# Stationary operands read with a step of two elements, and moving operands at other distances from them, in a conformer/state-space block

## The chip, the cores and the metric

The kernel runs on one core of one Trainium2 chip. The metric is the device time of one execution in microseconds. Five engines matter: TensorE (PE, matrix products, whose load of the stationary operand the profile lists apart as PEld), VectorE (DVE), ScalarE (ACT), GpSimd (POOL) and SyncE (SP), which here only issues DMAs.

## The reference, cut to what matters

One block of 512 tokens by 1024 features, everything in fp32. With `D = 1024`:

```python
h = rms_norm(x, mix_pre_g)
proj = h @ w_in                        # GLU halves, z, x/B/C, dt, gates
gates = sigmoid(proj[..., OFF_GATE:] + gate_b)
conv_out = conformer_conv_branch(...)  # GLU, 31-tap conv, layer norm, silu, @ pw_w
ssm_out = ssd_branch(...)              # 4-tap convs, chunked state space, group norm, @ ssm_out_w
mixed = (g_conv * conv_out + g_ssm * ssm_out) @ w_out
x = x + rms_norm(mixed, mix_post_g)
h = rms_norm(x, ffn_pre_g)
gt, up = split(h @ w_gate_up)
x = x + rms_norm((silu(gt) * up) @ w_down, ffn_post_g)
```

## The kernel before

**Three products for one.** An fp32 operand is held as two float32r tiles, a rounded high part and the remainder (`whi`/`wlo` for weights, `hhi`/`hlo`, `ehi`/`elo`, `yh`/`yl`, `vhi`/`vlo`, `mh`/`ml`, `fh`/`fl` for activations). `mm3` (lines 160 to 164) issues three matmuls per pair of tiles: high by high, stationary high by moving low, stationary low by moving high. Nearly all TensorE time is in these 5,448 matmuls (1,816 calls, the first strip's written out at lines 442 to 444).

**Weights.** `ORDER` lists 128 x 1024 pieces of the weights, laid out on the host by `_layout`. `w_raw` loads one from DRAM through the SP queue (five buffers, three ahead), `w_part` makes the high part with ACT and the low part with DVE, or with ACT and an accumulating DMA on the POOL queue. A piece is a strip of 128 output columns with its eight k tiles of 128 rows side by side; `proj` (line 190) takes columns `k*P` to `(k+1)*P` as the stationary operand and all 512 tokens as the moving one.

**The stages, in order.** (1) `val`/`glu` strips 0 to 7, strips 0 to 2 with `ehi`/`elo` as moving operand, the others with `hhi`/`hlo`; a 31-tap convolution follows on DVE, its taps fed out between later matmuls by `conv_some`, which ties each tap to the PE's progress. (2) Eight groups of the state-space branch: strips `x` (two), `B`, `C`, and `z` in `proj_z`, where the tokens in `hhi`/`hlo` are stationary and 256 columns of weights move; between them small fp32 matmuls (`s1` to `s4`) and the output product `ssm_out`, weights stationary and `yh`/`yl` moving. (3) Gates `gs` and `gc`, the layer norm of the convolution, and `pw` with `vhi`/`vlo` moving. (4) The product with `w_out` (`tm_step`): tokens in `mt` stationary, weights moving, then residual and norm in `residual`, and `transposed`, which writes the halves `b11` to `t4` in the `mov` tiles. (5) Gate and up projections in a seven-product form: 22 steps of 256 columns, `product` (line 848) takes a combination of weight quarters as stationary operand and one of seven combinations of activation halves (256 tokens) as moving one; four k tiles and three matmuls each. (6) The product with `w_down`: tokens in `fh`/`fl` stationary, weights moving.

**Where the tiles lie.** Taken modulo 512 bytes within a partition, the weight tiles (`whi`, `wlo`, `chi`, `clo`, `dhi`, `dlo`) begin at 160, and so do `ehi`, `elo`, `yh`, `yl`, `vhi`, `vlo`, the `mt` tiles, all `mov` tiles and the `f` tiles; `hhi` and `hlo` begin at 480. The unnamed tiles `place` and `mp_place` hold space only. The distance from a stationary to a moving operand, modulo 512 bytes, is thus 0 everywhere but with `hhi`/`hlo`: 320 where they move, 192 where they stand still in `proj_z`.

**Order of the work.** The Tile framework sets the order on each engine from the order of the calls, the explicit `keep_in_program_order`, `issue_after` and `not_before` edges, and the free buffers. [...]

Of the kernel before, what the change touches and what calls it, by code (L numbers as in the profile page):

```python
# [10 lines left out]
F32 = mybir.dt.float32  # L11
# [7 lines left out]
P = 128  # L19
# [77 lines left out]
ORDER += [("wd", _i) for _i in range(NF)]  # L97


def b3(ap, n):  # L100

    return ap.unsqueeze(len(ap.shape)).to_broadcast(list(ap.shape) + [n])
# [3 lines left out]
def block_kernel(ctx: ExitStack, tc: tile.TileContext, x, xT, prm, hp, gp, w, out):  # L106
# [83 lines left out]
    def proj(ps, wt, rhs=None):  # L190
        wh, wl = wt
        rhi, rlo = rhs or ([hhi[:, k, :] for k in range(NK)], [hlo[:, k, :] for k in range(NK)])
        for k in range(NK):
            c = slice(k * P, (k + 1) * P)
            mm3(ps, wh[:, c], wl[:, c], rhi[k], rlo[k], k == 0, k == NK - 1)

    sp = mid.enter_context(tc.tile_pool(name="mid", bufs=1))
# [227 lines left out]
    for j in range(NK):  # L425
        if j == EARLY:
            proj_z0()
            time_steps()
        if j == DT2:
            running_sums()  # L430
            L = {0: make_L(0)}
        if j == 1:
            pv, pg = [ydp.tile([P, T], F32, tag=f"yd{n}", name=f"p{n}_1") for n in range(2)]
        else:
            pv, pg = mm_tile(f"pv{j}"), mm_tile(f"pg{j}")
        early = (ehi, elo) if j < EARLY else None
        if j == 0:
            for k in range(NK):
                for ps, n in ((pv, "val"), (pg, "glu")):
                    wh, wl = w_get(n, 0)  # L440
                    c = slice(k * P, (k + 1) * P)
                    in_order(pe.matmul(ps, wh[:, c], ehi[k], start=k == 0, stop=False))
                    pe.matmul(ps, wl[:, c], ehi[k], start=False, stop=False)
                    pe.matmul(ps, wh[:, c], elo[k], start=False, stop=k == NK - 1)
            first = pv, pg
            continue
        proj(pv, w_get("val", j), early)
        if j == 1:
            with tc.issue_after(mark["pe"].ins):
                norm_x()  # L450
        proj(pg, w_get("glu", j), early)
        if j == 1:
            norm_to_all()
            gated(0, *first, True)
            norm_h()
        gated(j, pv, pg, early)
        if j >= EARLY - 1:
            conv_some(TAPS_GLU)
# [129 lines left out]
    def s4(g):  # L588
        s = st[g]
        yz = s["y"].rearrange("p c h d -> p c (h d)")  # L590
        if g % 2 == 0:
            ys[g // 2] = [ssd.tile([P, 4, T], F32R, tag=f"y{n}", name=f"y{n}{g}") for n in "hl"]
        yh, yl = ys[g // 2]
        for e in range(2):
            ps = aux_tile(f"pyT{g}_{e}")
            for c in range(NT):
                pe.transpose(ps[:, c * P : (c + 1) * P], yz[:, c, e * P : (e + 1) * P], ident)
            act.activation(yh[:, 2 * (g % 2) + e, :], ps, AF.Copy, scale=col("norm_g", 2 * g + e))
            dve.scalar_tensor_tensor(
                out=yl[:, 2 * (g % 2) + e, :], in0=ps, scalar=col("norm_g", 2 * g + e),  # L600
                in1=yh[:, 2 * (g % 2) + e, :].bitcast(F32), op0=ALU.mult, op1=ALU.subtract,
            )
        del st[g]

    def ssm_out(p, quarters):

        yh, yl = ys[p]
        for q in quarters:
            wh, wl = w_get("so", 4 * p + q)
            for i in (2 * q, 2 * q + 1):  # L610
                ps = mm_tile(f"pso{p}_{i}")
                for k in range(4):
                    c = slice(k * 256 + (i % 2) * P, k * 256 + (i % 2 + 1) * P)
                    mm3(ps, wh[:, c], wl[:, c], yh[:, k, :], yl[:, k, :], k == 0, k == 3)
                if p == 0:
                    act.copy(so[i], ps)
                else:
                    dve.tensor_tensor(out=so[i], in0=ps, in1=so[i], op=ALU.add)
# [53 lines left out]
    br.close()  # L672

    vp = mid.enter_context(tc.tile_pool(name="vT", bufs=1))
    vhi = vp.tile([P, NK, T], F32R, name="vhi")
    vlo = vp.tile([P, NK, T], F32R, name="vlo")
    gc = vp.tile([P, NK, T], F32, name="gc")
# [53 lines left out]
    mp = mix.enter_context(tc.tile_pool(name="mp", bufs=1, side="right"))  # L731
    M2 = T // 2
    mt = [[mp.tile([P, NK, M2], F32R, tag=f"m{n}{p}", name=f"m{n}{p}") for p in "hl"] for n in range(2)]
    mp.tile([P, 80], F32, name="mp_place")
    wo0 = seq[("wo", 0)]
    for i in range(NK):
        pw = mm_tile(f"ppw{i}")
# [52 lines left out]
    HB = T // 2  # L790
    KB = NK // 2
    MOV = ("b11", "b21", "b22", "t1", "t2", "t3", "t4")
    mov = {n: [h2p.tile([P, KB, HB], F32R, name=f"{n}{p}") for p in "hl"] for n in MOV}
    w2 = h2.enter_context(tc.tile_pool(name="w2", bufs=1))

    pm = ExitStack()
# [51 lines left out]
    def product(ps, u, wn, mn, start):  # L848

        wh, wl = forms[u, wn]  # L850
        mh, ml = mov[mn]
        for k in range(KB):
            c = slice(k * P, (k + 1) * P)
            mm3(ps, wh[:, c], wl[:, c], mh[:, k], ml[:, k], start and k == 0, k == KB - 1, not start)

    xrs, xgs = {}, {}

    def residual(t, ps):

        xr = pmp.tile([P, D], F32, tag="xr", name=f"xr{t}")  # L860
        nc.scalar.dma_start(xr, x[t * P : (t + 1) * P, :])
        mg = pmp.tile([P, D], F32, tag="mg", bufs=1, name=f"mg{t}")
        ss = []
        for n, c in enumerate(cols2):
            ss.append(mean_sq(ps[n], pmp, f"a{t}", n))
            dve.tensor_tensor(out=mg[:, c], in0=ps[n], in1=gpost0[:, c], op=ALU.mult)
        rs = factor(ss, f"a{t}")
        ss = []
        for n, c in enumerate(cols2):
            dve.scalar_tensor_tensor(out=xr[:, c], in0=mg[:, c], scalar=rs, in1=xr[:, c], op0=ALU.mult, op1=ALU.add)  # L870
            ss.append(mean_sq(xr[:, c], pmp, f"b{t}", n))
        rs = factor(ss, f"b{t}")
        dg = pmp.tile([P, P], F32, tag="dg", name=f"dg{t}")
        mark["dg"] = dve.tensor_scalar(out=dg, in0=ident, scalar1=rs, scalar2=None, op0=ALU.mult)
        xrs[t] = xr, dg
        nc.scalar.dma_start(x2d[t * P : (t + 1) * P, :], xr)

    def transposed(t):

        tok = slice((t // 2) * P, (t // 2 + 1) * P)  # L880
        xr, dg = xrs[t]
        xg = []
        for n in range(2):
# [44 lines left out]
    steps = [(t, k) for k in range(4) for t in (0, 1)] + [(t, k) for t in (0, 1) for k in range(4, NK)]  # L928
    steps += [(t, k) for t in (2, 3) for k in range(NK)]
    for t, k in steps:  # L930
        (mh, ml), tok = mt[t // 2], slice(t % 2 * P, (t % 2 + 1) * P)
        tm_step(ps, t, k, NK, mh[:, k, tok], ml[:, k, tok], split[wo0 + k])
        if k == NK - 1:
            residual(t, ps[t])
        if (t, k) == (2, 1):
            transposed(0)
            first_room = [mp.tile([P, 2, 1024], F32R, tag=f"m0{p}", name=f"a01{p}") for p in "hl"]
            for u in range(2):
                prep_a(u, [m[:, u] for m in first_room])
        if (t, k) == (2, 5):  # L940
            transposed(1)
        if (t, k) == (3, 1):
            hold += [mark["sq"], mark["dg"]]
            prep_a(2)
        if (t, k) == (3, 2):
            prep_a(3)
        if (t, k) == (3, 5):
            with tc.issue_after(mark["pe"].ins):
                transposed(2)
# [92 lines left out]

    def f_split(k):
        if k < NF and k not in fs:
            f_halves(k, [pf.tile([P, T], F32R, tag=f"f{p}", bufs=4, name=f"f{p}{k}") for p in "hl"])

    def f_step(ps, t, k, wt, ns=(0, 1)):
        tok = slice((t % 2 * 2 + t // 2) * P, (t % 2 * 2 + t // 2 + 1) * P)
        tm_step(ps, t, k, NF, fs[k][0][:, tok], fs[k][1][:, tok], wt, ns)

    ps = tm_tiles("wd")
# [10 lines left out]
    def store(t, mg, rs):  # L1062
        for n, c in enumerate(cols2):
            dve.scalar_tensor_tensor(
                out=x2[:, t, c], in0=mg[:, c], scalar=rs, in1=x2[:, t, c], op0=ALU.mult, op1=ALU.add
            )
            (nc.sync if n == 0 else nc.scalar).dma_start(out[t * P : (t + 1) * P, c], x2[:, t, c])

    for t in range(NT):
        mg = pf.tile([P, D], F32, tag="mg", name=f"mgc{t}")  # L1070
# [14 lines left out]
    return wt[:, cols].reshape(NK, P, -1).transpose(1, 0, 2).reshape(P, -1)  # L1085


def _layout(inp):
    x = inp["x"][0]
    w_in, pw, so = inp["w_in"][0], inp["conv_pw_w"][0], inp["ssm_out_w"][0]  # L1090
# [9 lines left out]
    def piece(n, i):  # L1100
        if n == "gu":
            u, j = i // 2, i % 2
            o = (u % 2) * FF + (u // 2) * 2 * P
            one, two = [_feature_major(wgu, slice(o + q * P, o + (q + 1) * P)) for q in range(2)]
            return one if j == 0 else two
        if n in strips:
            a, o = strips[n]
            return _feature_major(a, slice(o + i * P, o + (i + 1) * P))
        if n == "zd":
            a = zd[:, 3 * i : 3 * i + 3].reshape(P, -1)  # L1110
            return np.pad(a, ((0, 0), (0, D - a.shape[1])))
# [1 line left out]
            return zs[i // 2][:, (i % 2) * D : (i % 2 + 1) * D]  # L1113
        if n == "so":
            a = so[(i // 4) * 512 : (i // 4 + 1) * 512, (i % 4) * 256 : (i % 4 + 1) * 256]
            return a.reshape(4, P, 256).transpose(1, 0, 2).reshape(P, -1)
        return rows[n][i * P : (i + 1) * P]

    def cols(v):
# [37 lines left out]
```

## Time and profile before

| | us |
|---|---|
| median of 3 runs (lowest to highest) | 1088.03 (1087.17 to 1088.22) |
| span of the profiled execution | 1086.3 |
| its device time beyond that span, by the median | 1.7 |
| PE busy in the span | 1064.8 (98%) |
| PEld busy | 936.2 (86%) |
| DVE busy | 790.0 (73%) |
| ACT busy | 584.6 (54%) |
| POOL busy | 78.7 (7%) |

A matmul's time in the profile is from its start to the end of its results, and the next one starts well before that end. Busy PE time therefore doesn't say how fast the matmuls follow each other; the starts of successive ones do.

### The profile page before, as it was taken

To read this page: it belongs to the slowest core of one execution; us is meant where nothing else is said; L and a number is where in the kernel's file an instruction comes from. 1 tells how busy PE (TensorE), PEld (TensorE's weight loads), DVE (VectorE), ACT (ScalarE), POOL (GpSimd) and SP (SyncE) were. 2 spreads that over 40 slices of the span, in tenths; PEclk is the share of its full clock that TensorE was granted. 3 is DMA by queue.
4 is the path that set the end of the run, shared out by engine and by line. 5 is a ranking of instruction groups with operands and counts; after the bars stand their busy time and mean duration, and the time that the engine had idled before them with its cause. 6 is when DMAs were issued, how large, how long until landed. Compare 5 with 4: busy or idle time off the path is not lost.

```text
span 1086.3 us, 15679 instructions
## 1 busy us (share of the span) xinstructions
PE 1064.8 (98%) x6193; PEld 936.2 (86%) x6193; DVE 790.0 (73%) x1148; ACT 584.6 (54%) x955; POOL 78.7 (7%) x101
## 2 busy tenths in 40 slices
PE   8999999999999999999999999999999999999997
PEld 6888888988898889879888787888999999988886
DVE  6799995996698769697894365679988788643334
ACT  6657848595759465834323862466554554532222
POOL 2002001111111111100000000010000000000000
PEclk9999999999999999999999999999999999999999
DMA  8466553646535653452133222423342233353302
GB/s 284 116 175 213 147 126 97 175 117 194 135 98 140 171 136 98 117 136 78 40 106 112 74 97 78 174 98 117 116 137 98 87 127 98 117 186 105 97 1 78
DMA packets 37081, 132.98 MB, mean 122 GB/s; under 512 B 4368, under 2 KB 4624, under 8 KB 35984
## 3 DMA queue, kind: packets, MB, share of 16 engines
q1 hardware_dynamic: 28224, 97.31, 26.9%
q0 software_dynamic: 6048, 26.22, 11.3%
q10 hardware_dynamic: 2736, 8.46, 2.1%
q8 instruction: 48, 0.79, 0.3%
q14 instruction: 25, 0.20, 0.1%
HBM read 127.71 MB, written 4.26 MB: 121 GB/s over the span
## 4 chain that ended last, share of the span: by engine, by line
PE 77%; DVE 11%; ACT 4%; DMA 2%; issue 1%; POOL 1%; DVEq 0%; POOLq 0%; ACTq 0%
PE xy L162 4%; PE tm_wd L164 4%; PE tm_wd L162 4%; PE tm_wd L163 4%; PE xy L163 4%; PE xy L164 4%; PE pso L162 3%; PE pso L164 3%; PE pso L163 3%; PE yd L549 2%; DVE a L389 2%; DMA raw<-in_w 2%; PE px L163 2%; PE px L164 2%; PE px L162 2%; PE pz L162 2%
## 5 line engine op out<-in xcount | busy, mean ns | idle before, releaser
L129 ACT CAST whi<-raw 128x1024 fp32r<-128x1024 f32 (+1 forms) x134 | 137.7, 1035 | 214.0 <-PE pC L163 37.9
L389 DVE SCALAR_TENSOR_TENSOR a<-v,prm_t,a 128x485 f32<-128x485 f32 (+16 forms) x240 | 180.5, 756 | 4.2 <-ACT a L386 1.4
L134 DVE TENSOR_TENSOR wlo<-raw,whi 128x1024 fp32r<-128x1024 f32 (+1 forms) x100 | 119.3, 1198 | 52.6 <-ACT whi L129 52.5
L162 PE MATMUL pz<-whi,hhi 128*128 128x256 f32 (+1 forms) x256 | 73.6, 287 | 0.8 <-DVE sg L415 0.8
L163 PE MATMUL pz<-wlo,hhi 128*128 128x256 f32 (+1 forms) x256 | 72.2, 282 | 0.0
L164 PE MATMUL pz<-whi,hlo 128*128 128x256 f32 (+1 forms) x256 | 71.9, 281 | 0.0
L162 PE MATMUL tm_wd<-whi,fh 128*128 128x512 f32 x160 | 62.2, 389 | 0.0
L163 PE MATMUL tm_wd<-wlo,fh 128*128 128x512 f32 x160 | 62.2, 389 | 0.0
L164 PE MATMUL tm_wd<-whi,fl 128*128 128x512 f32 x160 | 62.2, 389 | 0.0
L820 DVE TENSOR_TENSOR wlo_g<-raw,whi_g 128x1024 fp32r<-128x1024 f32 x40 | 48.2, 1220 | 10.5 <-ACT whi_g L819 10.5
L819 ACT CAST whi_g<-raw 128x1024 fp32r<-128x1024 f32 x40 | 40.9, 1048 | 23.8 <-DVE raw L843 9.4
L162 PE MATMUL pso<-yh,whi 128*128 128x512 f32 x128 | 50.3, 394 | 0.6 <-DVE B L466 0.6
L164 PE MATMUL px<-hhi,wlo 128*128 128x512 f32 x128 | 50.5, 394 | 0.0
L1030 DVE TENSOR_TENSOR fl<-f,fh 128x512 fp32r<-128x512 f32 x20 | 13.8, 691 | 50.3 <-ACT fh L1029 50.3
L163 PE MATMUL px<-hlo,whi 128*128 128x512 f32 x128 | 50.4, 394 | 0.0
L164 PE MATMUL pso<-yh,wlo 128*128 128x512 f32 x128 | 50.2, 392 | 0.0
L132 POOL DMA_DIRECT2D wlo<-in_w x34 | 30.3, 891 | 273.3 <-ACT wlo L131 180.7
L162 PE MATMUL px<-hhi,whi 128*128 128x512 f32 x128 | 50.0, 391 | 0.0
L163 PE MATMUL pso<-yl,whi 128*128 128x512 f32 x128 | 50.0, 390 | 0.0
L162 PEld LDWEIGHTS pz<-whi,hhi 128*128 128x128 f32 x256 | 48.3, 189 | 1.3 <-DVE sg L415 1.0
L163 PEld LDWEIGHTS pz<-wlo,hhi 128*128 128x128 f32 x256 | 48.1, 188 | 0.3
L164 PEld LDWEIGHTS pz<-whi,hlo 128*128 128x128 f32 x256 | 48.2, 188 | 0.2
(430 smaller groups left out, 3230.5 us busy)
## 6 DMA issues: line engine op xcount, KB each, us to landing
raw<-in_w SPq DMA_DIRECT2D x177, 512.0 KB, 3.7
wlo<-in_w POOLq DMA_DIRECT2D x34, 512.0 KB, 5.3
L<-scr POOLq DMA_DIRECT2D x8, 1024.0 KB, 5.5
xT<-in_xT SPq DMA_DIRECT2D x8, 256.0 KB, 5.6
xr<-in_x ACTq DMA_DIRECT2D x4, 512.0 KB, 4.6
x2d<-xr ACTq DMA_DIRECT2D x4, 512.0 KB, 2.6
x<-x2d ACTq DMA_DIRECT2D x1, 2048.0 KB, 11.3
raw<-in_w SPq DMA_DIRECT2D x4, 256.0 KB, 4.7
```

What stands on the lines that cost most here:

```text
L129: act.copy(hi[:, c], src[:, c])
L132: pool.dma_start(lo[:, c], w[n][:, c].bitcast(F32R), accum_op=ALU.add)
L134: dve.tensor_tensor(out=lo[:, c], in0=src[:, c], in1=hi[:, c].bitcast(F32), op=ALU.subtract)
L162: mark["pe"] = pe.matmul(ps, lh, rh, start=start, stop=False, skip_group_check=more)
L163: pe.matmul(ps, lh, rl, start=False, stop=False, skip_group_check=more)
L164: pe.matmul(ps, ll, rh, start=False, stop=stop, skip_group_check=more)
L389: return dve.scalar_tensor_tensor(out=va[j][:, d:], in0=vs[j][:, : T - d], scalar=col("dw_w", j * KC + KC - 1 - d), in1=va[j][:, d:], op0= ...
L549: pe.matmul(yd[c // 2][:, c % 2, h, :], s["L"][:, h, c, :], s["xdt"][:, c, h, :], start=True, stop=True)
L819: a_ = act.copy(hi, src)
L820: d_ = dve.tensor_tensor(out=lo, in0=src, in1=hi.bitcast(F32), op=ALU.subtract)
L1030: dve.tensor_tensor(out=fs[k][1], in0=f32[:, k, :], in1=fs[k][0].bitcast(F32), op=ALU.subtract)
```

## The change

The stationary operand of most split products is read with a step of two elements instead of one. Strips are laid out on the host in pairs of k tiles, element by element in turn (`_paired`), and `pair(k)` names the columns of one of the two. The `so` weights are laid out the same way, with the two column halves in turn. Where tokens are stationary (`w_out`, `w_down`), each product takes every second token of 256, so that a result tile holds even or odd tokens; the residual is loaded and the output stored with the same step (`rows`), and `transposed` writes the `mov` tiles with it. `proj_z` and the small fp32 matmuls stay as they are.

Tiles that hold space only, and 64 bytes more at each of the `mov` and `f` tiles, move the operands: `yh`/`yl` by 256 bytes, `vhi`/`vlo` by 384, the `mt` tiles by 256; the 14 `mov` tiles begin 0, 64, 128, ... bytes further on (modulo 512, so that `b11h` and `t2h` stay where they were), and the four buffers each of `fh` and `fl` likewise. `ehi`/`elo` and `hhi`/`hlo` keep their distances of 0 and 320.

```diff
+def pair(k):
+    o = k // 2 * 2 * P
+    return slice(o + k % 2, o + 2 * P, 2)
...
# proj, the first strip, product
-            c = slice(k * P, (k + 1) * P)
+            c = pair(k)
...
# s4
+        if g == 0:
+            ssd.tile([P, 64], F32, name="y_place")
...
# ssm_out
-                    c = slice(k * 256 + (i % 2) * P, k * 256 + (i % 2 + 1) * P)
+                    c = slice(k * 256 + i % 2, (k + 1) * 256, 2)
...
+    vp.tile([P, 96], F32, name="v_place")
...
-    mp.tile([P, 80], F32, name="mp_place")
+    mp.tile([P, 16], F32, name="mp_place")
...
-    mov = {n: [h2p.tile([P, KB, HB], F32R, name=f"{n}{p}") for p in "hl"] for n in MOV}
+    mov = {}
+    for n in MOV:
+        mov[n] = [h2p.tile([P, KB * HB + 16], F32R, name=f"{n}{p}")[:, : KB * HB].rearrange("p (k t) -> p k t", k=KB) for p in "hl"]
+    h2p.tile([P, 32], F32, name="h2_place")
...
+    def rows(t):
+        return slice(t // 2 * 2 * P + t % 2, (t // 2 + 1) * 2 * P, 2)
...
-        nc.scalar.dma_start(xr, x[t * P : (t + 1) * P, :])
+        nc.scalar.dma_start(xr, x[rows(t), :])
...
# transposed
-        tok = slice((t // 2) * P, (t // 2 + 1) * P)
+        tok = slice(t // 2, HB, 2)
...
# w_out
-        (mh, ml), tok = mt[t // 2], slice(t % 2 * P, (t % 2 + 1) * P)
+        (mh, ml), tok = mt[t // 2], slice(t % 2, M2, 2)
...
-            f_halves(k, [pf.tile([P, T], F32R, tag=f"f{p}", bufs=4, name=f"f{p}{k}") for p in "hl"])
+            f_halves(k, [pf.tile([P, T + 16], F32R, tag=f"f{p}", bufs=4, name=f"f{p}{k}")[:, :T] for p in "hl"])
...
# w_down
-        tok = slice((t % 2 * 2 + t // 2) * P, (t % 2 * 2 + t // 2 + 1) * P)
+        tok = slice(t % 2 * HB + t // 2, (t % 2 + 1) * HB, 2)
...
-            (nc.sync if n == 0 else nc.scalar).dma_start(out[t * P : (t + 1) * P, c], x2[:, t, c])
+            (nc.sync if n == 0 else nc.scalar).dma_start(out[rows(t), c], x2[:, t, c])
...
+def _paired(wt, o):
+    return wt[:, o : o + P].reshape(NK // 2, 2, P, P).transpose(2, 0, 3, 1).reshape(P, -1)
```

## Rows read from the trace of the kernel before

**Rows 1.** The page: span, engines' busy time, granted clock in 40 slices, chain.
```profile
span 1086.3 us, 15679 instructions
PE 1064.8 (98%) x6193; PEld 936.2 (86%) x6193; DVE 790.0 (73%) x1148; ACT 584.6 (54%) x955; POOL 78.7 (7%) x101
PEclk9999999999999999999999999999999999999999
PE 77%; DVE 11%; ACT 4%; DMA 2%; issue 1%; POOL 1%; DVEq 0%; POOLq 0%; ACTq 0%
```
**Rows 2.** Waits of PE: who waited for whom, us in total, times, longest.
```profile
PE pxT L509 <- DVE yl L599: 2.9, 3, 1.5
PE ptr L886 <- DVE dg L874: 2.5, 1, 2.5
```
**Rows 3.** Timeline of PE (start us, us long, instruction), `w_down`, distance 0; 24 matmuls apart.
```profile
1000.19 0.39 PE L163 MATMUL tm_wd<-wlo,fh 128*128 128x512 f32 x1
...
1005.63 0.39 PE L163 MATMUL tm_wd<-wlo,fh 128*128 128x512 f32 x1
```
**Rows 4.** Timeline of PE, an `x` strip, distance 320; 15 matmuls apart.
```profile
222.05 0.39 PE L162 MATMUL px<-hhi,whi 128*128 128x512 f32 x1
...
225.48 0.39 PE L162 MATMUL px<-hhi,whi 128*128 128x512 f32 x1
```
**Rows 5.** Timeline of PE, gate and up products, distance 0; 11 matmuls apart.
```profile
861.73 0.28 PE L162 MATMUL v<-t1h,dhi 128*128 128x256 f32 x1
...
863.05 0.28 PE L164 MATMUL v<-t1h,dlo 128*128 128x256 f32 x1
```
**Rows 6.** Timeline of PE, `proj_z` of group 4, distance 192; 30 matmuls apart.
```profile
323.00 0.28 PE L163 MATMUL pz<-wlo,hhi 128*128 128x256 f32 x1
...
326.39 0.28 PE L163 MATMUL pz<-wlo,hhi 128*128 128x256 f32 x1
```
**Rows 7.** Timeline of PE, `proj_z` of group 3, distance 192; 27 matmuls apart.
```profile
282.09 0.28 PE L162 MATMUL pz<-whi,hhi 128*128 128x256 f32 x1
...
285.27 0.28 PE L162 MATMUL pz<-whi,hhi 128*128 128x256 f32 x1
```
**Rows 8.** Timeline of PE, fp32 matmuls of `s2`, two passes each, merged.
```profile
520.16 1.03 PE L539 MATMUL pSa<-xdec,BT 128*128 128x256 f32 x4
521.02 0.59 PE L539 MATMUL pSb<-xdec,BT 128*128 128x256 f32 x2
```
**Rows 9.** Timeline of PE, transposes of the layer norm: eight merged, and one alone.
```profile
550.63 1.03 PE L687 MATMUL pl<-ident,a 128*128 128x128 f32 x8
...
587.11 0.27 PE L687 MATMUL pl<-ident,a 128*128 128x128 f32 x1
```
**Rows 10.** Groups of PEld by line and form: busy us, mean ns, idle before them.
```profile
L162 PEld LDWEIGHTS px<-hhi,whi 128*128 128x128 f32 x128 | 24.1, 188 | 5.2
L162 PEld LDWEIGHTS v<-t1h,dhi 128*128 128x128 f32 x88 | 16.9, 192 | 0.0
```
**Rows 11.** Busy time of each engine in five stretches (us, instructions, clock, DMA share, GB/s).
```profile
41.00:109.00 68.00, 67.20 (x334) 56.91 (x334) 63.01 (x101) 45.94 (x67) 10.52 (x10) 1.00 0.62 171
192.00:488.00 296.00, 292.44 (x1690) 255.14 (x1689) 236.45 (x339) 188.53 (x306) 39.06 (x42) 1.00 0.52 138
488.00:560.00 72.00, 72.00 (x402) 61.65 (x402) 61.40 (x91) 24.74 (x44) 2.43 (x4) 1.00 0.21 68
712.00:780.00 68.00, 64.55 (x465) 60.91 (x464) 61.33 (x97) 42.98 (x83) 2.79 (x4) 0.97 0.30 103
780.00:981.00 201.00, 200.17 (x1573) 195.41 (x1573) 151.41 (x224) 96.80 (x158) 0.00 (x0) 1.00 0.36 122
```
**Rows 12.** Lines 900 and 901: ns shortest/median/longest, first and last start, forms.
```profile
L900 ACT CAST b11h<-xg x2: 637/639/641, 705.6 to 727.9; 128x512 fp32r<-128x512 f32 x2
L901 DVE TENSOR_TENSOR b11l<-xg,b11h x2: 689/691/693, 706.7 to 728.5; 128x512 fp32r<-128x512 f32 x2
```
**Rows 13.** The page, DMA issues: KB each, us to landing.
```profile
xr<-in_x ACTq DMA_DIRECT2D x4, 512.0 KB, 4.6
```

More of the change, by code (lines that the diff above doesn't have):

```diff
@@ L440, in block_kernel @@
                     wh, wl = w_get(n, 0)
-                    c = slice(k * P, (k + 1) * P)
+                    c = pair(k)
                     in_order(pe.matmul(ps, wh[:, c], ehi[k], start=k == 0, stop=False))
@@ L852, in product @@
         for k in range(KB):
-            c = slice(k * P, (k + 1) * P)
+            c = pair(k)
             mm3(ps, wh[:, c], wl[:, c], mh[:, k], ml[:, k], start and k == 0, k == KB - 1, not start)
     xrs, xgs = {}, {}
+    def rows(t):
+        return slice(t // 2 * 2 * P + t % 2, (t // 2 + 1) * 2 * P, 2)
     def residual(t, ps):
         xr = pmp.tile([P, D], F32, tag="xr", name=f"xr{t}")
-        nc.scalar.dma_start(xr, x[t * P : (t + 1) * P, :])
+        nc.scalar.dma_start(xr, x[rows(t), :])
         mg = pmp.tile([P, D], F32, tag="mg", bufs=1, name=f"mg{t}")
@@ L1103, in piece @@
             o = (u % 2) * FF + (u // 2) * 2 * P
-            one, two = [_feature_major(wgu, slice(o + q * P, o + (q + 1) * P)) for q in range(2)]
+            one, two = [_paired(wgu, o + q * P) for q in range(2)]
             return one if j == 0 else two
@@ L1107, in piece @@
             a, o = strips[n]
-            return _feature_major(a, slice(o + i * P, o + (i + 1) * P))
+            return _paired(a, o + i * P)
         if n == "zd":
@@ L1115, in piece @@
             a = so[(i // 4) * 512 : (i // 4 + 1) * 512, (i % 4) * 256 : (i % 4 + 1) * 256]
-            return a.reshape(4, P, 256).transpose(1, 0, 2).reshape(P, -1)
+            return a.reshape(4, P, 2, P).transpose(1, 0, 3, 2).reshape(P, -1)
         return rows[n][i * P : (i + 1) * P]
```

## The prediction

> **What bounds the kernel now.** [...] PE's waits are few: the two longest entries sum to 5.4 us [rows 2]. So the time is the matmul stream itself, and the question is at what pace it runs. The busy time can't answer that, since a matmul's bar is longer than the step to the next one; the starts can. For 512 moving columns, w_down shows 5.44 us for 24 matmuls, 226.7 ns each [rows 3]; the x strips 3.43 us for 15, 228.7 ns [rows 4]. For 256 columns, the gate and up products show 1.32 us for 11, 120.0 ns [rows 5], proj_z 113.0 ns in one group [rows 6] and 117.8 in another [rows 7].
>
> At one column per cycle of the full clock, 512 columns last 213.3 ns and 256 last 106.7. So each matmul loses 6 to 15 ns. Two rows tell what the least loss is. The fp32 matmuls of s2 make passes of 256 columns; four steps take 521.02 - 520.16 = 0.86 us, 215 ns each [rows 8], which is 512 cycles and 1.7 ns: a stream that also changes its stationary operand at each pass, at half the moving rate, and loses almost nothing. The transposes, with 128 moving columns (53 ns), follow each other every (1.03 - 0.27) / 7 = 0.109 us [rows 9]: there it is the load of 128 stationary columns that sets the step, so a load delivers a column in 0.85 ns, two cycles. A load's bar, 188 to 192 ns [rows 10], holds latency that overlaps; in the products the load engine has no idle time before its instructions, in the strips it has.
>
> From this I form the mechanism. The load for the next matmul runs beside the moving stream. With a step of one, the load walks 4 bytes in 0.85 ns and the stream 4 bytes in 0.42 ns: the stream overtakes the load, over 109 ns by some 512 bytes. The same shape runs at 120.0 ns at distance 0 and at 113.0 or 117.8 at distance 192 [rows 5 to 7], so part of the loss depends on where the operands lie, and on phase; s2, whose moving stream at half rate walks as fast as its load, loses nothing [rows 8]. I take the loss for the two reads meeting in the same part of the memory while one passes the other.
>
> **The change part by part.** A step of two makes the load walk 8 bytes in 0.85 ns: as fast as the stream. Then no passing takes place within a load, and the new distances keep the two apart from the start (256 for y, 384 for v, 256 for the mt tiles, 320 already for hhi; the mov and f tiles spread over all multiples of 64). The clock, the number of matmuls and the bytes from DRAM are unchanged.
>
> (a) Strips that read hhi/hlo: val and glu 3 to 7 (10), x (16), B, C, gs and gc (8 each) are 58 strips of 24 matmuls, 1,392. From 228.7 to 215 ns [rows 4, 8] is 13.7 ns: 19.1 us.
>
> (b) Other products with 512 columns: so 384, pw 192, w_out 192, w_down 528, together 1,296. From 226.7 to 215 [rows 3, 8] is 11.7 ns: 15.2 us.
>
> (c) Gate and up: 22 x 7 x 4 x 3 = 1,848 matmuls of 256 columns. The stream can't fall below 109 ns, since the load needs that [rows 9]; the best split matmuls of this shape stand at 113.0 [rows 6]. I take 113: 7.0 ns [rows 5], 12.9 us. The ends: nothing (some mov tiles keep distance 0) and 11 ns, 20.3 us.
>
> (d) The first three pairs of strips (144 matmuls) keep distance 0 with the new step. No row shows two full-rate streams locked at distance 0; if each loses as much again as now (13 ns) this is +1.9 us, if they run free -1.9. I take 0, nearest to s2, where an equal walk costs nothing.
>
> (e) transposed writes 14 mov pieces with ACT and 14 with DVE, 0.64 and 0.69 us each now [rows 12], with a step of two. No row has a stepped write. It could cost nothing or double: 28 x 0.67 = 18.8 us of engine time in a stretch where PE waits 2.5 us for that chain [rows 2]; half of it, 9 us, could then show. I take 0, because 512 elements in 0.69 us is one element at a time already, so a step has no burst to break.
>
> (f) The DMAs of x and out keep whole rows (4 KB and 2 KB) and change only the distance between them; the xr loads land in 4.6 us [rows 13] and are issued before the norms that need them. Zero; the host layout is outside the time.
>
> (g) What is given back. DVE is busy 63.0 of 68 us at 41:109, 61.4 of 72 at 488:560, 61.3 of 68 at 712:780, and 236 of 296 at 192:488 [rows 11]. None of these exceeds the shortened stretch (41:109 falls by about 3 us, to 65), but the slack halves there, and waits such as pxT for yl [rows 2] grow. Here (a) and (b) save about 9 us at 192:488, of which I give back 3; one more in each of the other three stretches: 6 us together. 780:981 has DVE at 151 of 201 [rows 11], and the change leaves room.
>
> Sum: 19.1 + 15.2 + 12.9 - 6 = 41 us off the profiled execution's span of 1086.3: 1045; with the 1.7 us by which the median of 1088.0 exceeds that span, 1047.
>
> On the load at a step of two, the rows only say what a step of one costs (109 ns). [...]
>
> **The rivals.** *Slower, the load costs by the memory it opens.* If the moving stream is held once for every piece of memory that the load touches, wherever both lie, a step of two doubles the pieces (1,024 bytes instead of 512) and with them the loss above the floor: (a) 13.7, (b) 11.7, (c) 11 ns once more: 19.1 + 15.2 + 20.3 = +54.6 us, 1143. For it: at 512 columns the loss hardly differs between distances 0 and 320 [rows 3, 4], and s2's freedom [rows 8] may come from its half-rate stream having time to spare. Against it: the same load and shape lose 6.3 ns or 13.3 by place and phase [rows 5, 6]. It decides as soon as the cost per load follows its extent.
>
> *Slower, the load itself slows.* If two cycles a column become four, the load needs 218 ns, hidden behind 512 columns only just, and it sets the pace of the 1,848 products: 98 ns each, +181 us, 1269. Against it: loads in 109 ns leave two cycles per column, so a single read per column keeps up.
>
> *No change.* If loads and streams don't meet at all, neither step nor place matters and the loss has another cause: 1088, give or take 6 for the moved tiles. Against it stand the rows at equal shape and different pace [rows 5 to 7]. [...]
>
> *Faster, but given back.* The pace improves as computed and DVE and ACT become the end of more waits, or only the 512-column matmuls gain: 34 us less twice the 6 us, 1066.
>
> **How the numbers follow.** The main forecast, with its weaker form, has 0.62; its own range is 1033 (all at the floor: 19.1 + 15.2 + 20.3 = 54.6 us and nothing given back, 1033) to 1066. No change has 0.13, spread over 1082 to 1094, about half of it within 0.2% (2 us, what a measurement of this kernel can tell from nothing) and the rest on both sides. The doubled loss has 0.20, the slow load 0.05. To hold 8 in 10 the range takes the forecast, the case of no change and the lower part of the doubled loss, a load that costs half as much again (27 us, 1115): 1032 to 1118. Faster 0.66, same 0.07, slower 0.27.
>
> **What would show each step.** In the trace after: starts of hhi strips and of w_down 215 to 217 ns apart for (a) and (b), 240 if the doubled loss is right, 227 to 229 if nothing happens. For (c), 109 to 114 ns; 131 under the doubled loss, 218 under the slow load; and a pace that differs between the seven forms, by their distance, if the place matters. For (d), strip pairs 1 and 2 against 3: worse at distance 0 than at 320 if lockstep at the same place hurts. For (e), lines 900 to 904 still at 0.64 to 0.69 us. For (g), PE's waits 6 us longer than now. The forecast fails if the load reads its columns in an order against the stream's: then a faster walk means more meetings, not none.

## The result: slower by one per cent, and the profile after

The changed kernel takes 1098.16 us (1097.35 to 1098.98 in four runs) against 1087.60 for the kernel before beside it (1085.61 to 1088.22): a ratio of 1.0099, with a 95% interval of 1.0084 to 1.0113. The forecast was a gain of 41 us; it is a loss of 10.6.

The page of the kernel after: span, busy time, granted clock, chain, as in [rows 1].

```profile
span 1096.9 us, 15679 instructions
PE 1076.5 (98%) x6193; PEld 956.8 (87%) x6193; DVE 791.0 (72%) x1148; ACT 584.8 (53%) x955; POOL 78.8 (7%) x101
PEclk9999999999999999999999999999999999999999
PE 80%; DVE 10%; ACT 3%; DMA 2%; issue 1%; POOL 1%; DVEq 0%; POOLq 0%; ACTq 0%
```

PE's busy time grew by 11.7 us and the span by 10.6; PE's idle time (span less busy) went from 21.5 to 20.4. DVE, ACT and POOL work as long as before, and the granted clock is the same (0.995 before, 0.996 after). So no new wait came; the matmul stream itself runs slower. PEld is busy 20.6 us longer (936.2 to 956.8), since a load with a step of two has a slightly longer bar, as the group of an `x` strip shows, before and after (ns shortest/median/longest, first and last start):

```profile
L162 PEld LDWEIGHTS px<-hhi,whi x128: 187/188/192, 116.1 to 448.2; 128*128 128x128 f32 x128
L168 PEld LDWEIGHTS px<-hhi,whi x128: 193/195/199, 117.1 to 451.2; 128*128 128x128 f32 x128
```

PE's waits in the kernel after (who waited for whom, us in total, times, longest) say the same as [rows 2]:

```profile
PE ptr L902 <- DVE dg L890: 2.5, 1, 2.5
PE pxT L515 <- DVE yl L607: 2.3, 3, 1.5
```

The timeline of PE after, in pairs of a first and a last start: an early strip at distance 0 (24 matmuls apart), the `x` strip of [rows 4] (15 apart), the products of [rows 5] (11 apart), and `w_down` [rows 3] over all its distances (117 apart).

```profile
9.25 0.39 PE L448 MATMUL pg<-ehi,whi 128*128 128x512 f32 x1
...
14.85 0.39 PE L448 MATMUL pg<-ehi,whi 128*128 128x512 f32 x1
...
224.16 0.40 PE L168 MATMUL px<-hhi,whi 128*128 128x512 f32 x1
...
227.66 0.40 PE L168 MATMUL px<-hhi,whi 128*128 128x512 f32 x1
...
869.51 0.28 PE L168 MATMUL v<-t1h,dhi 128*128 128x256 f32 x1
...
870.83 0.28 PE L170 MATMUL v<-t1h,dlo 128*128 128x256 f32 x1
...
984.61 0.40 PE L170 MATMUL tm_wd<-whi,fl 128*128 128x512 f32 x1
...
1011.78 0.40 PE L170 MATMUL tm_wd<-whi,fl 128*128 128x512 f32 x1
```

That is 233.3 ns for both strips (228.7 before), 120.0 for the products (120.0 before) and 232.2 for `w_down` (226.7 before). The bars themselves barely differ (0.39 or 0.40 us); only the starts show it.

The same reading was made for all successive starts of every kernel below. The table gives the mean step less 213.3 ns for 512 columns (106.7 for 256) as the loss of one matmul in ns. These two are an estimate: at distance 0 and a step of one, a matmul of 512 columns takes 226.7 ns [rows 3] and one of 256 takes 120.0 [rows 5], so 256 columns more take 106.7 ns more, 0.417 ns a column. No run has a step of 213.3 or 106.7 ns itself: the least in the table are 215.8 and 111.7. The table is worked out from the timelines; steps that hold a wait (more than 40 ns over; in the products at a step of four, more than 200) are left out. A step is counted for the matmul that begins it, and a distance is that between its moving operand and the next stationary one, whose load runs beside it (moving less stationary, modulo 512 bytes, as before). In the kernel before, the load for the next matmul starts with the first matmul of [rows 3], at 1000.19 us:

```profile
1000.19 0.19 PEld L164 LDWEIGHTS tm_wd<-whi,fl 128*128 128x128 f32 x1
```

| kernel | strips, `hhi`/`hlo` | early strips | `so` | `pw` | `w_out` | `w_down` | products (256) | `proj_z` (256) |
|---|---|---|---|---|---|---|---|---|
| matmuls in all | 1,392 | 144 | 384 | 192 | 192 | 528 | 1,848 | 672 |
| before | 16.4 | 15.4 | 14.4 | 13.6 | 13.7 | 13.4 | 13.2 | 8.7 |
| after | 20.0 | 19.8 | 20.0 | 18.1 | 20.6 | 18.9 | 13.2 | 8.2 |
| step two, old places | 20.0 | 19.8 | 19.9 | 20.0 | 19.9 | 22.2 | 13.3 | 8.2 |
| step one, new places | 16.4 | 14.4 | 14.4 | 19.0 | 13.7 | 17.3 | 12.4 | 8.7 |
| load of one column, 128 times | 18.2 | 15.8 | 17.9 | 18.3 | (14.0) | (13.4) | 8.2 | (8.2) |
| after, stream reversed | 20.0 | 19.9 | 21.0 | 20.0 | 21.9 | 20.0 | 12.0 | 11.1 |
| before, stream reversed | 20.0 | 18.3 | 20.1 | 20.0 | 20.0 | 20.0 | 11.7 | 11.2 |
| step four | 26.2 | 21.8 | 19.8 | 26.5 | 20.6 | 18.9 | 127 | (7.6) |
| stream standing still | 2.5 | 6.4 | 2.6 | 2.5 | 2.5 | 2.5 | 5.0 | 5.0 |
| stream at half pace | 2.5 | 6.2 | 2.5 | 2.5 | 2.5 | 2.5 | 5.0 | 5.0 |
| half the load | 15.3 | 16.0 | 16.0 | 16.0 | 15.9 | 16.4 | 9.4 | 8.4 |
| `mov` at 192 | 16.4 | 14.6 | 14.5 | 13.6 | 13.8 | 13.4 | 8.9 | 8.1 |
| `mov` at 192, `hhi`/`hlo` at 256 | 14.3 | 14.6 | 13.9 | 13.3 | 13.7 | 13.4 | 7.2 | 13.1 |

In brackets: places that the edit leaves alone. The first early strip is not written with `mm3` (lines 442 to 444 before), so the edits inside `mm3` leave it as it was, and the early column mixes two kinds there. (`so` and the two columns after it keep the step of two where others go to four.)

The table accounts for the result: strips 1,392 x 3.6 ns = 5.0 us, early strips 0.6, `so` 384 x 5.6 = 2.2, `pw` 0.9, `w_out` 1.3, `w_down` 528 x 5.5 = 2.9, products 0, `proj_z` -0.3: 12.6 us, beside the 11.7 by which PE's busy time grew.

### The profile page after: what moved, and what is told of

Its sections match the earlier page's. It is cut to its first block, busy times and chain, and to the rows that moved or that the text cites. A ratio compares the mean times of both kernels' runs of the same rounds, so it can differ in the third digit from the quotient of the medians.

```text
span 1096.9 us, 15679 instructions
## 1 busy us (share of the span) xinstructions
PE 1076.5 (98%) x6193; PEld 956.8 (87%) x6193; DVE 791.0 (72%) x1148; ACT 584.8 (53%) x955; POOL 78.8 (7%) x101
## 3 DMA queue, kind: packets, MB, share of 16 engines
q0 software_dynamic: 6048, 26.22, 11.4%
## 4 chain that ended last, share of the span: by engine, by line
PE 80%; DVE 10%; ACT 3%; DMA 2%; issue 1%; POOL 1%; DVEq 0%; POOLq 0%; ACTq 0%
PE tm_wd L170 4%; PE tm_wd L169 4%; PE tm_wd L168 4%; PE xy L168 4%; PE xy L169 4%; PE xy L170 3%; PE pso L168 3%; PE pso L170 3%; PE pso L169 3%; PE yd L555 2%; PE pz L168 2%; PE pz L170 2%; PE pz L169 2%; DVE a L395 2%; PE px L170 2%; PE px L168 2%
## 5 line engine op out<-in xcount | busy, mean ns | idle before, releaser
L1046 DVE TENSOR_TENSOR fl<-f,fh 128x512 fp32r<-128x512 f32 x20 | 13.8, 691 | 52.4 <-ACT fh L1045 52.4
```

The lines of the kernel that those rows point to most:

```text
L1046: dve.tensor_tensor(out=fs[k][1], in0=f32[:, k, :], in1=fs[k][0].bitcast(F32), op=ALU.subtract)
```

## The experiments

Four theories stood at the start. *Extent*: a load costs by the memory it opens (the rival of the prediction). *Places*: the new distances spoil what the old ones had. *Order*: load and stream pass each other or not by their direction and pace. *Walk*: the loss belongs to the stream's own pace, and what the load does only shades it. Medians of the kernel before beside the runs lie between 1086.9 and 1089.2 us.

### The step alone, at the old places

In the kernel after; `mov` and `f` tiles go back to their size of before as well:

```diff
-        if g == 0:
-            ssd.tile([P, 64], F32, name="y_place")
-    vp.tile([P, 96], F32, name="v_place")
-    mp.tile([P, 16], F32, name="mp_place")
+    mp.tile([P, 80], F32, name="mp_place")
```

> The step of two alone, all tiles where they lay before (distance 0, hhi/hlo 320). If the load's extent makes the loss: 512-column matmuls stay at 233 ns as in the changed kernel, 256-column ones at 120, time 1097 to 1100. If the moved tiles make it: back to 227 to 229 ns and 1088.

1099.54 us, ratio 1.0106 (1.0089 to 1.0123). The step alone costs all of it, and at distance 0 too: everywhere 20 ns, in `w_down` 22.2 (why more there, no run explains). The products, at distance 0 with a step of two, hold 120.0 ns as they did with a step of one. The new places therefore did not do the harm; in `w_down` (22.2 to 18.9) and `pw` (20.0 to 18.1) they took a little of it away.

### The places alone, at a step of one

In the kernel before; `mov` and `f` tiles get the 64 bytes more of the change as well:

```diff
+        if g == 0:
+            ssd.tile([P, 64], F32, name="y_place")
+    vp.tile([P, 96], F32, name="v_place")
-    mp.tile([P, 80], F32, name="mp_place")
+    mp.tile([P, 16], F32, name="mp_place")
```

> The places alone, step of one everywhere. If the extent makes the loss: 512-column matmuls at 226 to 230 ns, time 1085 to 1091. If the places make it: 233 ns and 1098. Either way the tiles at distances 0 to 448 give the loss of a step of one by distance, which the kernel before shows at 0, 192 and 320 only.

1089.30 us, ratio 1.0020 (1.0009 to 1.0030). By the table: `w_down` 528 x 3.9 = 2.1 us and `pw` 1.0 lost, products 1.5 gained; together 1.6, and 1.5 measured. With a step of one the distance matters. By distance (modulo 512 bytes) `w_down` loses 14.2 ns at 0, 18.3 at 64, 19.5 at 128, 20.7 at 192, 14.3 at 256, 15.3 at 320, 20.0 at 384, 19.9 at 448: low at 0 and 256, and not much higher at 320. The kernel before already had everything at 0 but what reads `hhi`/`hlo`.

`pw` was run at two distances with two steps. Its timeline, two starts 96 matmuls apart in each kernel; in the kernel before (step one, distance 0):

```profile
633.64 0.39 PE L163 MATMUL ppw<-vlo,whi 128*128 128x512 f32 x1
...
655.44 0.39 PE L163 MATMUL ppw<-vlo,whi 128*128 128x512 f32 x1
```

The same with the places alone (step one, 384):

```profile
635.16 0.39 PE L162 MATMUL ppw<-vhi,whi 128*128 128x512 f32 x1
...
657.46 0.40 PE L162 MATMUL ppw<-vhi,whi 128*128 128x512 f32 x1
```

With the step alone (step two, 0):

```profile
640.06 0.39 PE L168 MATMUL ppw<-vhi,whi 128*128 128x512 f32 x1
...
662.46 0.39 PE L168 MATMUL ppw<-vhi,whi 128*128 128x512 f32 x1
```

And in the kernel after (step two, 384):

```profile
639.37 0.40 PE L168 MATMUL ppw<-vhi,whi 128*128 128x512 f32 x1
...
661.59 0.40 PE L168 MATMUL ppw<-vhi,whi 128*128 128x512 f32 x1
```

227.1, 232.3, 233.3 and 231.5 ns. One of the four is low, and it is the one that the kernel before had.

### A load that stands still

In the kernel before, in strips and products; `so` is edited likewise:

```diff
-            c = slice(k * P, (k + 1) * P)
-            mm3(ps, wh[:, c], wl[:, c],
+            mm3(ps, same(wh, k * P), same(wl, k * P),
...
+def same(ap, o):
+    return ap[:, o : o + 1].to_broadcast([P, P])
```

> The kernel before with a stationary operand that reads one column 128 times (a step of zero) in the strips, the so and the gate and up products; w_out and w_down as before. The sums are then not the block's, the work is as much. If what the load walks over makes the loss: 215 ns for 512 columns and 109 to 113 for 256, w_down still 227, time 1040 to 1050. If a load costs the same whatever it reads: 227 to 229 and 120 ns, time 1088.

1086.32 us, one run; neither reading's paces came. The load reads a single column, and the 512-column matmuls lose more than with a step of one: the `x` strip goes at 231.3 ns (timeline, first pair, 15 matmuls apart), `pw` at distance 0 loses 18.3 instead of 13.6. `w_down`, untouched, stays at 226.7 (second pair, 24 apart).

```profile
222.81 0.40 PE L167 MATMUL px<-hhi,whi 128*128 128x512 f32 x1
...
226.28 0.39 PE L167 MATMUL px<-hhi,whi 128*128 128x512 f32 x1
...
984.66 0.39 PE L167 MATMUL tm_wd<-whi,fh 128*128 128x512 f32 x1
...
990.10 0.39 PE L167 MATMUL tm_wd<-whi,fh 128*128 128x512 f32 x1
```

*Extent* falls with this: one column in place of 128, and the loss is nearly that of a step of two (18.2 ns in the strips against 20.0). So does its opposite, that the load's walk is what has to be got out of the way. Nor is it the longer bar of a load with a step of two: here, as in the reversed run at a step of one below, the strips' loads keep a median bar of 188 ns, and the strips lose 18 and 20 ns. The products did gain (13.2 to 8.2 ns), so for 256 columns what the load reads has a part.

### The stream turned round

In `mm3`, once of the kernel after and once of the kernel before:

```diff
+        rh, rl = [r[:, ::-1] for r in (rh, rl)]
```

> The changed kernel with every moving operand of a split product read back to front (the columns of each product then stand in reverse, so what is computed after them is not the block). If the load walks against the stream now, both walk the same way at the same pace here: 512-column matmuls at 215 to 220 ns at distances other than 0, time 1040 to 1060. If only the extent counts: 233 ns, time 1098.

> The kernel before (step of one, old places) with every moving operand of a split product read back to front; the columns of each product stand in reverse, so what follows is not the block. If the small loss of 13.5 ns at distance 0 and 512 columns depends on which way the stream walks beside the load, it goes to the 20 ns that every other pairing shows: 233 ns, 1095 to 1100. If the direction doesn't matter: 227 to 229 ns, 1088.

1099.29 and 1098.08 us, one run each. The timeline of `w_down`, starts 24 matmuls apart, with a step of two:

```profile
984.61 0.40 PE L171 MATMUL tm_wd<-whi,fl 128*128 128x512 f32 x1
...
990.21 0.40 PE L171 MATMUL tm_wd<-whi,fl 128*128 128x512 f32 x1
```

And with a step of one:

```profile
984.79 0.40 PE L164 MATMUL tm_wd<-wlo,fh 128*128 128x512 f32 x1
...
990.39 0.40 PE L164 MATMUL tm_wd<-wlo,fh 128*128 128x512 f32 x1
```

Both 233.3 ns, 20 ns of loss. With the stream reversed, step and distance stop mattering for 512 columns: `w_down` with a step of two loses 19.9 to 20.1 ns at each of its eight distances (`so` and `w_out` with a step of two, at 21 to 22, are off, and the early column, a third of which the edit leaves alone). *Order* had two readings; in one of them, a load that runs against the stream, turning the stream round should have freed step two, and it did not. What is left of it is that direction does matter: the low at distance 0 needs a stream that runs forwards (`w_down` at a step of one loses 13.4 ns forwards and 20.0 reversed).

### A step of four

In the kernel after, in `pair`, and in `_paired` on the host likewise; four k tiles lie element by element in turn:

```diff
-    o = k // 2 * 2 * P
-    return slice(o + k % 2, o + 2 * P, 2)
+    o = k // 4 * 4 * P
+    return slice(o + k % 4, o + 4 * P, 4)
```

> The changed kernel with four k tiles in turn, a step of four in the strips and the gate and up products (so and tokens stay at two). If a step other than one only loses the favourable pairing: strips at 232 to 234 ns, products at 119 to 120, time 1097 to 1101. If the loss follows the extent of the load: strips at 240 ns or more, over 1105. [...]

1315.70 us, one run. Here the load itself slows. Two groups of the tile `v` by line and operation (ns shortest/median/longest, first and last start):

```profile
L168 PEld LDWEIGHTS v<-t1h,dhi x88: 329/330/333, 774.6 to 1175.1; 128*128 128x128 f32 x88
L168 PE MATMUL v<-t1h,dhi x88: 393/395/401, 774.7 to 1175.2; 128*128 128x256 f32 x88
```

The timeline of the products, 11 apart:

```profile
899.80 0.40 PE L169 MATMUL v<-t1l,dhi 128*128 128x256 f32 x1
...
902.37 0.40 PE L168 MATMUL xy<-t3h,chi_g 128*128 128x256 f32 x1
```

The load's bar is 330 ns instead of 192 [rows 10], and a product starts every 233.6 ns instead of 120: the load sets the step, at about twice the 109 ns of [rows 9]. Neither reading of the expectation has this; the prediction's rival of the slow load had it, for a step of two and at 218 ns. The strips, where the load has 512 columns to hide behind, lose 26 ns.

The products with a step of two kept their 120.0 ns: there the load's bar grew from 192 to 197 ns (medians of `v<-t1h,dhi`), but it doesn't set a slower step. Why a step of four slows the load and a step of two does not, no run shows.

### A stream that stands still

In `mm3` of the kernel before, the first column is read as often as there are columns:

```diff
+        n = rh.shape[1]
+        rh, rl = [r[:, :1].to_broadcast([P, n]) for r in (rh, rl)]
```

> The kernel before with a moving operand that reads its first column 256 or 512 times in every split product but the first strip's; what is computed is not the block. If the loss comes from the stream's reads meeting the load's: 215 to 217 ns for 512 columns, 109 to 112 for 256, time 1030 to 1045. If the load alone sets it: 227 and 120 ns, 1088.

1052.75 us, one run. The timeline of `w_down`, 24 apart:

```profile
984.67 0.38 PE L164 MATMUL tm_wd<-whi,fh 128*128 128x512 f32 x1
...
989.85 0.38 PE L164 MATMUL tm_wd<-whi,fh 128*128 128x512 f32 x1
```

215.8 ns, a loss of 2.5, in every stage of 512 columns but the early strips; the products lose 5.0. With the same loads as before, at the same step and the same clock (0.993 granted, 0.995 before), nearly all of the loss is gone. It comes only with a stream that walks; whether it takes the load beside it as well, this run can't say. The paces are those of the first reading; the time is above its 1030 to 1045, since PE's busy time fell by 47.6 us and the span by 35.3 only.

### A stream at half pace

In `mm3` of the kernel before, each of the first half of the columns is read twice:

```diff
+        n = rh.shape[1] // 2
+        rh, rl = [r[:, :n].unsqueeze(2).to_broadcast([P, n, 2]) for r in (rh, rl)]
+        ps = ps.rearrange("p (n r) -> p n r", r=2)
```

> The kernel before with a moving operand that reads each of its first 256 (128) columns twice, so that the stream takes a column per cycle but walks 2 bytes per cycle instead of 4, as fast as a load with a step of one; all split products but the first strip's, and what is computed is not the block. If the loss belongs to the pace of the stream's walk: close to the 215.8 and 111.7 ns of the standing moving operand, 1050 to 1056. If an equal walk of load and stream is as bad as in the changed kernel: 232 ns and 1095. If the stream's pace doesn't matter as long as it walks: 227 and 120 ns, 1088.

1054.60 us, one run. Still 512 columns, and the operand advances 4 bytes in two of them: 0.84 ns at the pace below, as the stream of `s2` does with 215 ns for 256 columns [rows 8]. The timeline of `w_down`, 24 apart:

```profile
984.74 0.38 PE L166 MATMUL tm_wd<-wlo,fh 128*128 128x512 f32 x1
...
989.92 0.38 PE L166 MATMUL tm_wd<-wlo,fh 128*128 128x512 f32 x1
```

PE's three longest waits in it (who waited for whom, us in total, times, longest):

```profile
PE pxT L512 <- DVE yl L602: 6.3, 4, 2.6
PE ptr L889 <- issue: 6.2, 3, 4.5
PE xy L165 <- DVE sg L980: 2.7, 3, 1.5
```

Again 215.8 ns, as if it stood still. This run was to tell two readings of `s2` apart: free because load and stream walk equally fast, or free because its stream is slow. Half pace with a load at a step of one is an equal walk, and free; full pace with a load at a step of two is an equal walk too, and loses 20 ns (the kernel after). Equal walks are thus not the condition. A stream that is slow or stands is in all three free cases (`s2`, and this run and the last). The granted clock of 0.995 is that of the kernel before.

The waits answer another term of the forecast. PE's busy time fell from 1064.8 to 1017.1 us, by 47.7, the span only by 33.5 (1086.3 to 1052.8): 14.2 us were given back as waits, with `pxT` waiting 6.3 us instead of 2.9 and `ptr` 6.2 instead of 2.5.

### Half the load

In `mm3` of the kernel before, in all but the first and last call of a sum:

```diff
+        if not start and not stop:
+            ps, lh, ll = ps[:64], lh[:, :64], ll[:, :64]
```

> The kernel before with a stationary operand of 64 columns instead of 128 in every split product but the first and last of a sum (their result rows 64 to 127 miss those terms); the moving columns are as many. If the loss of a 512-column matmul beyond the 2.5 ns that a standing moving operand leaves comes from the load beside it: about half of 11 ns, 220 to 222 ns, and 256 columns, no more held by the load, at 110 to 114 ns; time 1050 to 1065. If the stream's own walk makes it: 227 and 120 ns, 1088.

1083.47 us, one run; neither reading's paces came. The load did shorten, from a bar of 188 to 134 ns. The timeline of `w_down`, 24 apart:

```profile
984.63 0.39 PE L164 MATMUL tm_wd<-whi,fh 128*64 128x512 f32 x1
...
990.15 0.39 PE L164 MATMUL tm_wd<-whi,fh 128*64 128x512 f32 x1
```

That is 230.0 ns, more than before. In the table the strips lose 1.1 ns less than before, the other 512-column matmuls 0.6 to 3.0 more, and the products fall from 13.2 to 9.4. But the edit makes two things half as wide, the load and the matmul that uses it, and the ends of each sum, where they differ, hold them apart. In `pw`, `w_out` and `w_down` together a matmul of 128 stationary columns loses 14.1 ns beside a full load and 12.8 beside half a load (20 steps); one of 64 columns loses 17.3 and 16.6. In the products it is 13.1 and 10.8, and 6.8 and 8.1. So half the load alone takes off 1.3 of 14 ns at 512 columns, far from half, and 2.3 of 13 at 256. The rest of what these matmuls lost or gained goes with the narrower matmul itself.

### Finer distances, and `mov` at 192

Both in the kernel before, at a step of one. In the first, the `mov` pairs begin at 96, 128, ... 288 and the `f` pairs at 0, -32, -64 and -96; in the second, all `mov` tiles at 192:

```diff
-    mov = {n: [h2p.tile([P, KB, HB], F32R, name=f"{n}{p}") for p in "hl"] for n in MOV}
+    mov = {}
+    h2p.tile([P, 24], F32, name="h2_first")
+    for n in MOV:
+        hi = h2p.tile([P, KB, HB], F32R, name=f"{n}h")
+        lo = h2p.tile([P, KB * HB + 8], F32R, name=f"{n}l")[:, : KB * HB].rearrange("p (k t) -> p k t", k=KB)
+        mov[n] = [hi, lo]
...
```

```diff
+    h2p.tile([P, 48], F32, name="h2_first")
     mov = {n: [h2p.tile([P, KB, HB], F32R, name=f"{n}{p}") for p in "hl"] for n in MOV}
+    h2p.tile([P, 80], F32, name="h2_place")
```

> The kernel before, step of one, with the seven pairs of mov tiles at distances 96 to 288 in steps of 32 (high and low part alike) and the four pairs of f tiles at 0, -32, -64 and -96. If the distance alone sets the pace: one clear figure for each, least near 192 for 256 columns (113 to 118 ns) and 120 or more away from it; for 512 columns least at 0 (227 ns), 230 to 234 elsewhere; time 1083 to 1092.

> The kernel before, step of one, all mov tiles 192 bytes further on, so that every gate and up product has the distance at which proj_z stands. If distance sets the pace of 256-column products: 113 to 118 ns instead of 120, 2 to 7 ns on 1,848 matmuls, 1075 to 1084. If proj_z is faster for another reason: 120 ns, 1088.

Finer distances: 1088.26 us, one run. `w_down` loses 14.5 ns at 0, 19.6 at -32, 19.9 at -64 and 20.6 at -96: the low for 512 columns is narrow. The products (the seven forms) lose 13.3 at 96, 12.2 at 128, 11.7 at 160, 10.6 at 192, 11.4 at 224, 12.6 at 256 and 10.2 at 288: a shallow low near 192, which is where `proj_z` stands, and 288 off that trend.

All `mov` tiles at 192: 1081.83 us, ratio 0.9944 (0.9928 to 0.9961). The products lose 8.9 ns, as `proj_z` does: 1,848 x 4.3 = 7.9 us, of which 5 show in the time.

### The low for each width

As the last, and `hhi`/`hlo` moved by 64 bytes:

```diff
     hlo = hp_pool.tile([P, NK, T], F32R, tag="lo", name="hlo")
+    hp_pool.tile([P, 16], F32, name="h_place")
```

> The mov tiles at distance 192 as in the run before, and hhi/hlo at 256 instead of 320 (256 instead of 192 in proj_z). 1,392 matmuls of 512 columns from 229.5 to 227.5 ns give 3 to 4 us; proj_z, 672 matmuls, may lose 1 to 3 us by leaving 192. Time 1078 to 1082; 1084 or more if proj_z loses more than the strips gain.

1080.02 us, ratio 0.9923 (0.9904 to 0.9942): 7.4 us below the kernel before and 18 below the changed one. The timeline of an `x` strip at distance 256 (15 apart), a `proj_z` (27 apart) and products (11 apart):

```profile
222.20 0.40 PE L162 MATMUL px<-hhi,whi 128*128 128x512 f32 x1
...
225.62 0.39 PE L162 MATMUL px<-hhi,whi 128*128 128x512 f32 x1
...
320.32 0.28 PE L164 MATMUL pz<-whi,hlo 128*128 128x256 f32 x1
...
323.55 0.28 PE L164 MATMUL pz<-whi,hlo 128*128 128x256 f32 x1
...
919.75 0.28 PE L164 MATMUL v<-t1h,dlo 128*128 128x256 f32 x1
...
920.99 0.28 PE L163 MATMUL xy<-t3l,whi_g 128*128 128x256 f32 x1
```

228.0, 119.6 and 112.7 ns. This strip is one of the slower ones; over all strips the loss fell from 16.4 to 14.3, 2.9 us. `proj_z`, which holds the same tiles still, moved from its low at 192 to 256 and pays 672 x 4.4 = 3.0 against the kernel before, 3.4 against the run with `mov` at 192 (8.1 to 13.1 ns). The strips' gain is thus spent. The products' loss fell further, from 8.9 to 7.2, with the same distance; that was not meant, and no run explains it. The intervals of the last two ratios overlap, so that this kernel beats the one with `mov` at 192 is not shown; that both beat the kernel before is.

## Why the prediction was wrong, point by point

**What bounds the kernel** held: the time is the pace of the matmul stream, and PE's busy time moved by 11.7 us with a span that moved by 10.6. The method, starts instead of bars, is the one that shows the result. The 213.3 and 106.7 ns from which the losses are counted agree with the difference between [rows 3] and [rows 5], but as the step of a matmul no run shows them. One reading needs a second row: [rows 9] can't tell load from stream by itself, since 128 columns at the pace of `s2` (215 ns for 256) last 107.5 ns as well. The `yd` matmuls of the kernel before tell them apart: with 64 moving columns the merged row below still has a step of (3.68 - 0.28) / 31 = 0.110 us, so the load sets it. Half the load says the same, with a bar 54 ns shorter for 64 columns fewer, 0.84 ns a column.

```profile
522.38 3.68 PE L549 MATMUL yd<-xdt,L 128*128 128x64 f32 x32
```

**The mechanism failed, and it failed in one step**: from [rows 8] it was taken that `s2` is free because its load and its stream walk equally fast. `s2` differs from the split products in two things at once, the equal walk and the slow stream, and no row of the trace before held them apart. The run at half pace and the kernel after do: the slow stream is free (215.8 ns), the equal walk at full pace loses 20 ns, more than the unequal one had. So the prediction's sentence that with equal walks no passing takes place, and with it no loss, is the one that fell. The time of 1098 lies within its 1032 to 1118 only because that range took in the lower part of the doubled loss, whose cause the runs don't show either.

**(a) and (b)** rested on that step alone. For 215 ns they show 233.3 and 231 to 234: instead of -19.1 us about +5.0, and instead of -15.2 about +7.3 (`so` 2.2, `pw` 0.9, `w_out` 1.3, `w_down` 2.9). The kernel before wasn't at an average place that any change could improve: with a step of one, 512 columns and a forward stream, the loss is low at distances 0 and 256 and 15 to 21 ns at the others, and (b) stood in that low already. The step of two has no such low (17.1 to 20.6 ns at the eight distances of `w_down` in the kernel after, 20 to 22 at distance 0 with the step alone), so it gave up what was there; the strips, at 320, stood at 16.4, and lost 3.6 too.

**(c)**: 120.0 ns instead of 113 (119.6 to 120.3 by form, so the spread of the forms by distance is small); 0 instead of -12.9 us, the lower end of its own bounds. No row showed that a load at a step of two is as fast as at a step of one; with 120.0 ns in both kernels, it is at least not slower than the products' step. The products can reach 113 [rows 6], but by distance (192), not by step.

**(d)** early strips at distance 0: the same 233.3 ns as the others at 320. Lockstep at the same place neither helps nor hurts; the term was put at 0 and measures 144 x 4.4 = 0.6 us, inside its bounds of 1.9.

**(e) and (f)** held. The stepped writes of `transposed` after, lines 916 and 917, answer [rows 12]:

```profile
L916 ACT CAST b11h<-xg x2: 669/670/671, 713.2 to 735.5; 128x512 fp32r<-128x512 f32 x2
L917 DVE TENSOR_TENSOR b11l<-xg,b11h x2: 687/691/695, 714.2 to 736.2; 128x512 fp32r<-128x512 f32 x2
```

0.67 us on ACT instead of 0.64, 0.69 on DVE unchanged, and `ptr` waits 2.5 us as before: a step of two in a write costs 5% on one engine and nothing on the path. For (f), the `xr` loads land in 4.9 us instead of 4.6 [rows 13], and no wait of PE ends on a DMA.

**(g)** didn't arise, as there was no gain. It was undersized, though: where a like gain was made (47.7 us of PE time at half pace), 14 us came back as waits, against 6 of 47 in the sum. By that (an estimate), the time would have been some 1055, not 1047, had the mechanism held.

**The rivals.** *The doubled loss* has the sign but not the cause: it asked for 54.6 us and a loss that follows what the load touches, but beside a load that touches one column the loss is nearly that of a step of two (17.9 to 18.3), half a load takes off a tenth of it and not half, and the products at a step of two lose nothing more. *The load itself slows* is what happens at a step of four (233.6 ns a product), not at two (120.0). *No change* had the reason "neither step nor place matters", and both matter. The sentence on what would make the forecast fail, a load that reads against the stream, is not the answer either: with the stream reversed, step two stays at 20 ns.

The load doesn't leave the stream's pace alone: the same 512-column shape runs at 226.7 to 235.5 ns by step, distance and direction, and the step of the stationary operand by itself takes `w_down` from 226.7 to 235.5 ns. The loss isn't what the prediction made of it either.

**What stays open.** Why a stream at full pace loses 13 to 20 ns at all, and by what the load's step, the distance and the direction shade it. That it is the distance and not each operand's own place is likely: with the roles exchanged, `proj_z` and the products lose 8.7 and 8.9 ns at 192, 13.1 and 12.6 at 256. But the products also lost 10.6 and 7.2 at 192 in two other runs, so the distance isn't the whole of it. Whether such a stream would lose as much with no load beside it wasn't tried. Nor was a stationary operand read in blocks of several columns.

## What to carry to other kernels

Before a layout is changed to heal a loss, find out by a run or two which of the two operands the loss belongs to: holding the moving operand still, and then letting it run at half pace, would have shown here that the loss goes with the stream's pace, with the load unchanged beside it. A row that differs from the case at hand in two things (`s2`: equal walk and half rate) supports no term of a sum until a run has held them apart. And where matmuls follow each other without waits, the distance between stationary and moving operand is a cheap thing to try, at each width by itself: three unused tiles gave 0.8%.

## What the runs showed of the hardware that was not expected

- A 512-column float32r matmul with its load at a step of one takes about 227 ns at distance 0 or 256, 228.7 to 234 at the others, and 215.8 when its moving operand stands still or advances every second column, with the same loads beside it (granted clock 0.993 to 0.996).
- Reversing the moving operand of 512 columns gives 233.3 ns at nearly every distance and either step, and takes the low at 0 away.
- At a step of two the load of 128 fp32 columns has a bar of 192 to 201 ns instead of 186 to 193 (all but a few), and products keep their 120.0 ns; at four the load sets their step, at 233.6 ns.
- For 256 columns the low lies near 192 bytes (113.9 to 117.3 ns in the mean), for 512 at 0 and 256; what suits the strips doesn't suit `proj_z`, which reads the same tiles in the other role.
